# A hybrid decoder step: the clamp of the SSD decay matrix, by eight ScalarE Relus with a bias and a negated Exp

## The chip, the cores and the metric

The program runs on one core of one Trainium2 chip. The metric is the time of one execution on the device in microseconds, the median of several. Five engines work side by side, each with its own queue of instructions that it carries out strictly in order: PE (TensorE, matrix products), DVE (VectorE), ACT (ScalarE), POOL (GpSimd) and SP (SyncE, which here only issues DMAs). They wait for each other by semaphores.

## The reference

One layer with two branches over a prompt of 2048 tokens and a small sample batch: sliding-window attention, and a Mamba-2 state-space scan (SSD). The edited lines belong to the scan of the prompt, in chunks of 128 tokens, 32 heads in 4 groups:

```python
a_cs = jnp.cumsum(dts * A.reshape(SSD_GROUPS, SSD_HPG), axis=2)
seg = a_cs[:, :, :, None] - a_cs[:, :, None]
Lm = jnp.exp(jnp.where(causal[:, :, None, None], seg, -jnp.inf))
cb = jnp.einsum('bclgn,bcsgn->bclsg', Cs, Bs)
y_diag = jnp.einsum('bclsg,bclsgh,bcsghp->bclghp', cb, Lm, dx)
...
y_off = jnp.einsum('bclgn,bcghpn,bclgh->bclghp', Cs, h_prev, jnp.exp(a_cs))
```

`Lm` is the decay matrix of a head: the exponent of the difference of two cumulative sums, for l >= s only. `a_cs` falls along the chunk, so below the diagonal the difference is never positive, and a clamp at zero changes nothing there; above it the clamp keeps the exponent finite, and the product with the masked `cb` makes it zero.

## The kernel before

The kernel has three stages. The first (`phase_t1`) projects q, k, v and does the attention; the second (`phase_s`) is the state-space branch; the third (`phase_t2`) does the output projections, with the sample batch in between. The prompt is cut into four blocks `b` of 512 tokens, each block into four chunks `c` of 128.

In `phase_s` each of the 4 x 4 pairs of block and head group first goes through `proj_group`: ten projections of 24 products each (`L181`, 128x512), which are drained by ACT (`L742`, `L743`) and convolved by DVE (`L748`, three per tile); the weights come by DMA (`raw`), and ACT and DVE split them into a high and a low part (`whl`, `L147`, `L148`). Then `ssd_group` does the scan. For each of its four chunks, with eight heads:

- `AB` is the cumulative sum of the eight heads along the free axis, spread over all partitions by a DMA; `acs` holds the same sums with a token per partition. Line 843, eight times on DVE, one head each, forms `min(AB - acs, 0)` in `L`; line 844 on ACT takes the exponent of all eight; line 845 on POOL multiplies by the masked product `cbm`. `AB` and `L` have two buffers each.
- `EB` is the sum again, spread over half the partitions by two DMAs (`L850`), its exponent taken on ACT (`L851`) and multiplied on DVE (`L855`) by `po`, the product of C with the state `H` (`L854`, on PE).
- PE transposes x (`L858`), DVE scales it twice (`dx`, `wx`, `L861` and `L862`), PE multiplies `dx` by `L` (`py`, `L866`). `wx` is split on ACT and POOL (`ws`, `L868`, `L869`), and PE forms the chunk's state product `st` from it (`L872`, three products).
- POOL decays the state (`hd`, `L878`), DVE adds the new part (`H`, `L879`); the next chunk's `po` needs this `H`. The output is summed by POOL and DVE (`L881`, `L882`, `L884`, `L885`).

After the four chunks the output is squared on ACT (`L887`), summed and split on DVE (`L888` to `L892`, `thl`), and two products on PE (`L895`) give the sums over partitions.

No queue is written out by hand. The framework schedules the whole program at compile time with a cost model of its own and so fixes the order of each engine's instructions: the products of the next group's projections stand between the small products of this group's scan. At run time each engine keeps to that order and waits where its input is late.

Of the kernel before, what the change touches and what calls it, by code (L numbers as in the profile page):

```python
# [11 lines left out]
AF = mybir.ActivationFunctionType  # L12
ALU = mybir.AluOpType
# [62 lines left out]
def build(tc, nc, a, o, seq, phases=("T1", "S", "T2"), dbg=None):  # L76
    NB = seq // TB
    V, A, G, PE, SY = nc.vector, nc.scalar, nc.gpsimd, nc.tensor, nc.sync
# [67 lines left out]
    def split(hi, lo, src, **kw):  # L146
        A.copy(hi, src)  # L147
        V.tensor_tensor(lo, src, hi.bitcast(F32), ALU.subtract)  # L148
# [557 lines left out]
    def phase_s():  # L706
        with ExitStack() as es:
# [115 lines left out]
            def ssd_group(b, g, xT, BT, CT, zs, dt, acs, dec, wd):  # L823
                tr = trp.tile([P, NT, P], F32, name="tr", tag="tr")
                for c in range(NT):
                    PE.transpose(tr[:, c], BT[:, c * P : (c + 1) * P], ident)
                Bt = ck.tile([P, 2, NT, P], F32R, name="Bt", tag="Bt", bufs=1)
                split(Bt[:, 0], Bt[:, 1], tr)
                pcb = trp.tile([P, NT, P], F32, name="tr", tag="tr")
                for c in range(NT):  # L830
                    sl = slice(c * P, (c + 1) * P)
                    PE.matmul(pcb[:, c], BT[:, sl], CT[:, sl], start=True, stop=True)
                cbm = ck.tile([P, NT, P], F32, name="cbm", tag="cbm")
                V.tensor_tensor(cbm, pcb, tri.unsqueeze(1).to_broadcast([P, NT, P]), ALU.mult)  # L834
                for c in range(NT):
                    first = b == 0 and c == 0
                    sl = slice(c * P, (c + 1) * P)
                    hc = slice(c * 32 + 8 * g, c * 32 + 8 * g + 8)
                    AB = lp.tile([P, 8, P], F32, name="AB", tag="AB")
                    SY.dma_start(AB.rearrange("p h l -> p (h l)"), ac_d[b][hc].rearrange("h l -> (h l)").partition_broadcast(P))  # L840
                    L = lp.tile([P, 8, P], F32, name="L", tag="L")
                    for h in range(8):
                        V.tensor_scalar(L[:, h], AB[:, h], acs[:, hc.start + h : hc.start + h + 1], 0.0, ALU.subtract, ALU.min)  # L843
                    A.activation(L, L, AF.Exp)  # L844
                    G.tensor_tensor(L, L, cbm[:, c].unsqueeze(1).to_broadcast([P, 8, P]), ALU.mult)  # L845
                    if not first:
                        EB = lp.tile([P, 4, P], F32, name="EB", tag="EB")
                        for hl in range(2):
                            src = ac_d[b][hc].rearrange("(i l) t -> l i t", l=2)[hl]
                            SY.dma_start(EB[64 * hl : 64 * hl + 64], src.partition_broadcast(64))  # L850
                        A.activation(EB, EB, AF.Exp)  # L851
                        po = yop.tile([P, 4, P], F32, name="po", tag="po")
                        for i in range(4):
                            PE.matmul(po[:, i], H[g][:, i * P : (i + 1) * P], CT[:, sl], start=True, stop=True)  # L854
                        V.tensor_tensor(EB, po, EB, ALU.mult)  # L855
                    tr = trp.tile([P, 8, 64], F32, name="tr", tag="tr")
                    for i in range(4):
                        PE.transpose(tr[:, 2 * i : 2 * i + 2].rearrange("p h d -> p (h d)"), xT[:, i, sl], ident)  # L858
                    dx = ck.tile([P, 8, 64], F32, name="dx", tag="dx")
                    wx = ck.tile([P, 8, 64], F32, name="wx", tag="wx", bufs=1)  # L860
                    V.tensor_tensor(dx, tr, dt[:, hc].unsqueeze(2).to_broadcast([P, 8, 64]), ALU.mult)  # L861
                    V.tensor_tensor(wx, tr, wd[:, hc].unsqueeze(2).to_broadcast([P, 8, 64]), ALU.mult)  # L862
                    py = yp.tile([P, 4, P], F32, name="py", tag="py")
                    for i in range(4):
                        for hl in range(2):
                            PE.matmul(py[64 * hl : 64 * hl + 64, i], dx[:, 2 * i + hl], L[:, 2 * i + hl], start=True, stop=True)  # L866
                    ws = ck.tile([P, 2, 8, 64], F32R, name="ws", tag="ws", bufs=1)
                    A.copy(ws[:, 0], wx)  # L868
                    G.tensor_tensor(ws[:, 1], wx, ws[:, 0].bitcast(F32), ALU.subtract)  # L869
                    pst_ = stp.tile([P, 8, 64], F32, name="st", tag="st")  # L870
                    for n, (x, y) in enumerate(SPLIT3):
                        PE.matmul(pst_, Bt[:, x, c], ws[:, y], start=n == 0, stop=n == 2)  # L872
                    Hg = H[g].rearrange("p (h d) -> p h d", h=8)
                    if first:
                        V.tensor_copy(Hg, pst_)
                    else:
                        hd = ck.tile([P, 8, 64], F32, name="hd", tag="hd", bufs=1)
                        G.tensor_tensor(hd, Hg, dec[:, hc].unsqueeze(2).to_broadcast([P, 8, 64]), ALU.mult)  # L878
                        V.tensor_tensor(Hg, pst_, hd, ALU.add)  # L879
                    u = xT[:, :, sl]  # L880
                    G.tensor_tensor(u, u, Dcol[:, 4 * g : 4 * g + 4].unsqueeze(2).to_broadcast([P, 4, P]), ALU.mult)  # L881
                    V.tensor_tensor(u, py, u, ALU.add)  # L882
                    if not first:
                        G.tensor_tensor(u, u, EB, ALU.add)  # L884
                    V.tensor_tensor(zs[:, :, sl], zs[:, :, sl], u, ALU.mult)  # L885
                SY.dma_start(v_d[b][g].rearrange("c p t -> p c t"), zs)
                A.activation(xT, zs, AF.Square)  # L887
                V.tensor_tensor(xT[:, :2], xT[:, :2], xT[:, 2:], ALU.add)  # L888
                V.tensor_tensor(xT[:, 0], xT[:, 0], xT[:, 1], ALU.add)
                thl = sqp.tile([P, 2, TB], F32R, name="thl", tag="thl")  # L890
                V.tensor_copy(thl[:, 0], xT[:, 0])
                V.tensor_tensor(thl[:, 1], xT[:, 0], thl[:, 0].bitcast(F32), ALU.subtract)  # L892
                pss = stp.tile([32, TB], F32, name="st", tag="st")
                for i in range(2):
                    PE.matmul(pss, onesr, thl[:, i], start=i == 0, stop=i == 1)  # L895
                sm = sqp.tile([1, TB], F32, name="sm", tag="sm")
                A.copy(sm, pss[:1])
                SY.dma_start(ss_d[b][g], sm)
# [8 lines left out]
            for b in range(NB):  # L907
                dts_ = dt_block(b)
                hT = load_h(b, b == sb)
                for g in range(4):  # L910
                    ssd_group(b, g, *proj_group(b, g, hT), *dts_)
                    stats(b, g)
# [404 lines left out]
```

## Time and profile before

| | |
|---|---|
| median of 3 runs | 3275.4 us (3272.0 to 3277.6) |
| span of the profiled execution, first to last instruction | 3273.9 us |
| the median of the runs less that span | 1.5 us |
| PE busy | 3130.4 us, 96% |
| DVE busy | 2234.8 us, 68% |
| ACT busy | 1308.2 us, 40% |
| POOL busy | 1045.0 us, 32% |
| first and last start of line 843 | 850.1 and 2050.3 us |
| first and last start of line 887, once in each of 16 groups | 909.5 and 2064.3 us |

The profile is of one execution, and its own time is the span; what a run spends before the first and after the last instruction is not in it. Busy time of PE is counted to the modelled end of each product, and products overlap, so a busy PE may still do less than its best; a PE that is not busy is waiting. A stretch from one start of line 887 to the next is one group of the SSD stage. The granted clock is the share of full speed that the throttle gave TensorE.

### The profile page before, as it was taken

How to read it: one execution, taken by the hardware profiler on the slowest of the kernel's cores; microseconds unless marked ns; L12 is line 12 of the kernel's file. 1: busy time of each engine (PE TensorE's matmuls, PEld its weight loads, DVE VectorE, ACT ScalarE, POOL GpSimd, SP SyncE). 2: the span in 40 equal slices, each digit the busy share in tenths (PEclk: the TensorE clock that was granted, in tenths of full speed). 3: DMA queues.
4: the chain of work that ended last, by engine and by line, in shares of the span. 5: the costliest groups of instructions: out<-in, count | busy, mean ns of one | idle time of the engine just before them, and what ended most of it. 6: DMA issues, size and time to landing. Idle time of an engine off the chain costs nothing.

```text
span 3273.9 us, 49350 instructions
## 1 busy us (share of the span) xinstructions
PE 3130.4 (96%) x19038; PEld 2656.9 (81%) x19038; DVE 2234.8 (68%) x3777; ACT 1308.2 (40%) x2334; POOL 1045.0 (32%) x965
## 2 busy tenths in 40 slices
PE   6999999999989999998999999999999999999999
PEld 5978787878878877776777777788877799999888
DVE  3777768678887798989888898555555554334433
ACT  3555535456344344434444444332333333222322
POOL 1534343443445455556554555200211110000000
PEclk8999999999999999999999999999999999999999
DMA  6544425323433444444344433444764574345443
GB/s 210 156 134 124 128 73 169 106 70 124 130 122 110 154 125 135 126 156 133 116 143 155 127 118 119 154 141 117 229 184 142 131 226 147 97 135 168 132 116 101
DMA packets 472788, 448.76 MB, mean 137 GB/s; under 512 B 33808, under 2 KB 420520, under 8 KB 472504
## 3 DMA queue, kind: packets, MB, share of 16 engines
q1 hardware_dynamic: 472552, 445.60, 44.9%
q8 instruction: 150, 2.46, 0.3%
q14 instruction: 86, 0.70, 0.1%
HBM read 382.26 MB, written 65.35 MB: 137 GB/s over the span
## 4 chain that ended last, share of the span: by engine, by line
PE 63%; DVE 24%; DMA 5%; POOL 3%; issue 3%; ACT 2%; SPq 1%; DVEq 0%; ACTq 0%; POOLq 0%
PE mm L181 37%; PE mm L192 11%; DVE acc L748 5%; DVE L L843 5%; PE mm L168 5%; DVE whl L148 3%; PE tr L547 3%; PE sc L519 2%; POOL L L845 2%; DVE zs L885 1%; DMA v<-v_d 1%; PE tr L536 1%; DVE xT L882 1%; DVE H L879 1%; DMA hT<-h_d 1%
## 5 line engine op out<-in xcount | busy, mean ns | idle before, releaser
L181 PE MATMUL mm<-hT,whl 128*128 128x512 f32 (+1 forms) x6720 | 1353.7, 357 | 19.8 <-DMA hT<-h_d 9.9
L181 PEld LDWEIGHTS mm<-hT,whl 128*128 128x128 f32 x6720 | 1122.0, 190 | 194.0 <-issue 22.9
L148 DVE TENSOR_TENSOR whl<-raw,whl 128x2048 fp32r<-128x2048 f32 (+1 forms) x232 | 522.7, 2256 | 261.7 <-ACT whl L147 255.4
L181 PE MATMUL mm<-ot,whl 128*128 128x512 f32 (+1 forms) x2880 | 571.7, 356 | 1.2 <-DVE whl L148 0.8
L181 PEld LDWEIGHTS mm<-ot,whl 128*128 128x128 f32 x2880 | 476.1, 189 | 74.0 <-issue 5.7
L147 ACT CAST whl<-raw 128x2048 fp32r<-128x2048 f32 (+1 forms) x232 | 412.7, 1787 | 250.1 <-PE mm L181 133.9
L192 PE MATMUL mm<-whl,hT 128*128 128x256 f32 (+1 forms) x2304 | 305.6, 288 | 16.2 <-ACT whl L147 12.8
L192 PEld LDWEIGHTS mm<-whl,hT 128*128 128x128 f32 x2304 | 288.6, 190 | 24.4 <-ACT whl L147 13.0
L748 DVE SCALAR_TENSOR_TENSOR acc<-cr,cwb,acc 128x512 f32<-128x512 f32 x288 | 274.9, 960 | 10.4 <-ACT acc L743 5.0
L845 POOL TENSOR_TENSOR L<-L,cbm 128x1024 f32<-128x1024 f32 x64 | 200.2, 3138 | 115.3 <-DVE cbm L834 57.9
L192 PE MATMUL mm<-whl,ot 128*128 128x256 f32 (+1 forms) x1632 | 203.9, 284 | 0.0
L192 PEld LDWEIGHTS mm<-whl,ot 128*128 128x128 f32 (+1 forms) x1632 | 197.6, 188 | 5.3 <-issue 4.9
L168 PE MATMUL mm<-hT,whl 128*128 128x512 f32 x768 | 195.1, 403 | 6.0 <-DVE zs L418 3.7
L843 DVE TENSOR_SCALAR L<-AB,acs 128x128 f32<-128x128 f32 x512 | 192.0, 443 | 0.0
L168 PEld LDWEIGHTS mm<-hT,whl 128*128 128x128 f32 x768 | 142.6, 191 | 42.0 <-issue 5.2
L844 ACT ACTIVATE L<-L 128x1024 f32<-128x1024 f32 x64 | 67.8, 1062 | 187.8 <-DVE L L843 187.8
L365 ACT ACTIVATE s<-s,ng 128x128 f32<-128x128 f32 x256 | 100.0, 394 | 59.9 <-DVE ng L359 57.7
L147 ACT CAST ot<-v 128x512 fp32r<-128x512 f32 x96 | 59.0, 621 | 158.4 <-DVE v L1183 79.9
L752 ACT ACTIVATE th<-acc 128x512 f32<-128x512 f32 x96 | 60.6, 632 | 145.4 <-DVE acc L748 145.3
L869 POOL TENSOR_TENSOR ws<-wx,ws 128x512 fp32r<-128x512 f32 x64 | 102.5, 1601 | 44.4 <-ACT ws L868 44.4
L540 POOL TENSOR_TENSOR PT<-PT 128x512 f32<-128x512 f32 x60 | 78.2, 1308 | 92.6 <-DVE PT L539 78.9
L1183 DVE SCALAR_TENSOR_TENSOR v<-v,snw,rb 128x512 f32<-128x512 f32 x64 | 48.0, 770 | 84.7 <-DMA v<-v_d 84.7
(320 smaller groups left out, 3964.3 us busy)
## 6 DMA issues: line engine op xcount, KB each, us to landing
raw<-in_w_in_dram SPq DMA_DIRECT2D x120, 1024.0 KB
hT<-h_d SPq DMA_DIRECT2D x80, 512.0 KB
raw<-in_w_in_dram SPq DMA_DIRECT2D x64, 512.0 KB
AB<-ac_d SPq DMA_DIRECT2D x64, 512.0 KB
raw<-in_w_ssd_proj_dram SPq DMA_DIRECT2D x32, 1024.0 KB
v_d<-zs SPq DMA_DIRECT2D x16, 1024.0 KB
v<-v_d SPq DMA_DIRECT2D x64, 256.0 KB
raw<-in_w_attn_proj_dram SPq DMA_DIRECT2D x64, 256.0 KB
```

What stands on the lines that cost most here:

```text
L147: A.copy(hi, src)
L148: V.tensor_tensor(lo, src, hi.bitcast(F32), ALU.subtract)
L168: PE.matmul(ps, hl[:, x, k, c0 : c0 + P], ht[:, y, :], start=first and i == 0, stop=last and i == n - 1,)
L181: PE.matmul(ps, hl[:, x, k, c0 : c0 + P], ht[:, y, lo : lo + n], start=i == 0, stop=i == 3 * len(hT) - 1,)
L192: PE.matmul(ps, ht[:, x, tt * P : tt * P + m], hl[:, y, k, :n], start=i == 0, stop=i == 3 * len(hT) - 1,)
L365: A.activation(s[:, i, :width], s[:, i, :width], AF.Exp, bias=ng[:, i : i + 1], accum_out=den[:, i : i + 1])
L540: G.tensor_tensor(PT[:, 0], PT[:, 0], PT[:, 1], ALU.subtract)
L547: PE.matmul(po[64 * kvl : 64 * kvl + 64], vT[:, tt + w, kv * HD : (kv + 1) * HD], PTs[kvl][:, w], start=w == ws[0], stop=w == 1,)
L748: V.scalar_tensor_tensor(out=acc, in0=raw[:, k : k + TB], scalar=cwb[:, k, ct : ct + 1], in1=acc, op0=ALU.mult, op1=ALU.add)
L843: V.tensor_scalar(L[:, h], AB[:, h], acs[:, hc.start + h : hc.start + h + 1], 0.0, ALU.subtract, ALU.min)
L845: G.tensor_tensor(L, L, cbm[:, c].unsqueeze(1).to_broadcast([P, 8, P]), ALU.mult)
L869: G.tensor_tensor(ws[:, 1], wx, ws[:, 0].bitcast(F32), ALU.subtract)
```

## The change

The eight instructions of line 843 go from DVE to ACT. Each is a Relu of `-AB + acs`, which is `-min(AB - acs, 0)`, with the column of `acs` as the bias of each partition; the exponent takes the negative by its scale. Nothing else in the source changes.

```diff
--- before.py
+++ after.py
@@ -840,8 +840,8 @@
                     SY.dma_start(AB.rearrange("p h l -> p (h l)"), ac_d[b][hc].rearrange("h l -> (h l)").partition_broadcast(P))
                     L = lp.tile([P, 8, P], F32, name="L", tag="L")
                     for h in range(8):
-                        V.tensor_scalar(L[:, h], AB[:, h], acs[:, hc.start + h : hc.start + h + 1], 0.0, ALU.subtract, ALU.min)
-                    A.activation(L, L, AF.Exp)
+                        A.activation(L[:, h], AB[:, h], AF.Relu, scale=-1.0, bias=acs[:, hc.start + h : hc.start + h + 1])
+                    A.activation(L, L, AF.Exp, scale=-1.0)
                     G.tensor_tensor(L, L, cbm[:, c].unsqueeze(1).to_broadcast([P, 8, P]), ALU.mult)
                     if not first:
                         EB = lp.tile([P, 4, P], F32, name="EB", tag="EB")
```

The scheduler lays the whole SSD stage out anew. Three places show it; all are in the third head group (`H_8613`) of a later block, which repeats almost unchanged from group to group.

The first is on PE, in the middle of a group: from the end of the state product of the first chunk (`st`) to the `po` of the third. `mm` are products of the projections. Before:

```order
L181 MATMUL mm<-hT,whl 128x512 x13
L858 MATMUL tr<-cst,xT 128x128 x4
L866 MATMUL py<-L,dx 64x128 x8
L181 MATMUL mm<-hT,whl 128x512 x5
L854 MATMUL po<-CT,H_8613 128x128 x4
L872 MATMUL st<-ws,Bt 128x512 x3
L181 MATMUL mm<-hT,whl 128x512 x8
L866 MATMUL py<-L,dx 64x128 x8
L181 MATMUL mm<-hT,whl 128x512 x28
L854 MATMUL po<-CT,H_8613 128x128 x4
```

And now:

```order
L181 MATMUL mm<-hT,whl 128x512 x13
L858 MATMUL tr<-cst,xT 128x128 x4
L866 MATMUL py<-L,dx 64x128 x5
L854 MATMUL po<-CT,H_8613 128x128 x4
L866 MATMUL py<-L,dx 64x128 x3
L872 MATMUL st<-ws,Bt 128x512
L181 MATMUL mm<-hT,whl 128x512 x6
L872 MATMUL st<-ws,Bt 128x512 x2
L181 MATMUL mm<-hT,whl 128x512 x16
L866 MATMUL py<-L,dx 64x128 x8
L181 MATMUL mm<-hT,whl 128x512 x8
L854 MATMUL po<-CT,H_8613 128x128 x4
```

Between one chunk's `st` and the next chunk's `po`, which needs the updated `H`, stand fewer products than before: 18 and then 36 before, 13 and then 24 now (the last six products ahead of the rest of `st` are not counted).

The second place is the end of the same group, on PE and on DVE. PE before, from the `st` of the third chunk to the product on `thl`:

```order
L872 MATMUL st<-ws,Bt 128x512 x3
L866 MATMUL py<-L,dx 64x128 x8
L181 MATMUL mm<-hT,whl 128x512 x20
L854 MATMUL po<-CT,H_8613 128x128 x4
L872 MATMUL st<-ws,Bt 128x512 x3
L181 MATMUL mm<-hT,whl 128x512 x66
L895 MATMUL st<-thl,onesr 32x512
```

PE now:

```order
L872 MATMUL st<-ws,Bt 128x512 x3
L181 MATMUL mm<-hT,whl 128x512 x11
L866 MATMUL py<-L,dx 64x128 x8
L181 MATMUL mm<-hT,whl 128x512 x5
L854 MATMUL po<-CT,H_8613 128x128 x4
L872 MATMUL st<-ws,Bt 128x512
L181 MATMUL mm<-hT,whl 128x512 x4
L872 MATMUL st<-ws,Bt 128x512 x2
L181 MATMUL mm<-hT,whl 128x512 x61
L895 MATMUL st<-thl,onesr 32x512
```

From `st` to the fourth `po` there are 16 `mm` in place of 20; from that `po` to `thl` 65 in place of 66.

DVE before, at the same place (`L843` is the edited line, `whl` the split of a weight, `L855` the product with `EB`, `L885` the last sum of a chunk):

```order
L882 TENSOR_TENSOR xT<-py,xT 128x4x128
L843 TENSOR_SCALAR L<-AB,acs 128x128 x8
L748 SCALAR_TENSOR_TENSOR acc<-cr,cwb,acc 128x512
L885 TENSOR_TENSOR zs<-zs,xT 128x4x128
L148 TENSOR_TENSOR whl<-raw,whl 128x2048
L748 SCALAR_TENSOR_TENSOR acc<-cr,cwb,acc 128x512
L753 SCALAR_TENSOR_TENSOR xT<-th,acc 128x512
L855 TENSOR_TENSOR EB<-po,EB 128x512
L879 TENSOR_TENSOR H_8613<-st,hd 128x512
L748 SCALAR_TENSOR_TENSOR acc<-cr,cwb,acc 128x512 x2
L885 TENSOR_TENSOR zs<-zs,xT 128x4x128
```

DVE now:

```order
L882 TENSOR_TENSOR xT<-py,xT 128x4x128
L855 TENSOR_TENSOR EB<-po,EB 128x512
L879 TENSOR_TENSOR H_8613<-st,hd 128x512
L748 SCALAR_TENSOR_TENSOR acc<-cr,cwb,acc 128x512
L885 TENSOR_TENSOR zs<-zs,xT 128x4x128
L748 SCALAR_TENSOR_TENSOR acc<-cr,cwb,acc 128x512
L148 TENSOR_TENSOR whl<-raw,whl 128x2048
L748 SCALAR_TENSOR_TENSOR acc<-cr,cwb,acc 128x512
L888 TENSOR_TENSOR xT<-xT 128x1024
```

The eight of `L843` are gone, and the split `L148` that stood ahead of the last `EB` and `H` now stands behind them and behind `L885`.

The third place is on ACT and on SP, in such a group. ACT before, from the tanh of a convolution (`L752`) to the second exponent (`L844`) after it:

```order
L752 ACTIVATE th<-acc 128x512
L868 CAST ws<-wx 128x512
L844 ACTIVATE L<-L 128x1024
L742 COPY cr<-mm 128x512
L743 ACTIVATE acc<-mm,cwb 128x512
L147 CAST whl<-raw 128x2048
L851 ACTIVATE EB<-EB 128x512
L844 ACTIVATE L<-L 128x1024
```

ACT now:

```order
L752 ACTIVATE th<-acc 128x512
L843 ACTIVATE L<-AB,acs 128x128 x8
L868 CAST ws<-wx 128x512
L844 ACTIVATE L<-L 128x1024
L742 COPY cr<-mm 128x512
L743 ACTIVATE acc<-mm,cwb 128x512
L147 CAST whl<-raw 128x2048
L851 ACTIVATE EB<-EB 128x512
L843 ACTIVATE L<-AB,acs 128x128 x8
L868 CAST ws<-wx 128x512
L844 ACTIVATE L<-L 128x1024
```

The eight Relus stand in a row, ahead of the cast of `ws`, the exponent and the draining of the projections (`L742`, `L743`).

SP before, the loads of one group:

```order
L840 DMA AB<-ac_d_93 128x1024
L850 DMA EB<-ac_d_93 64x4x128 x2
L840 DMA AB<-ac_d_93 128x1024
L154 DMA raw<-in_w_in_dram 128x8x256
L850 DMA EB<-ac_d_93 64x4x128 x2
L840 DMA AB<-ac_d_93 128x1024
L850 DMA EB<-ac_d_93 64x4x128 x2
L840 DMA AB<-ac_d_93 128x1024
L154 DMA raw<-in_w_in_dram 128x8x128 x2
L850 DMA EB<-ac_d_93 64x4x128 x2
L886 DMA v_d_2_82<-zs 128x4x512
```

SP now:

```order
L840 DMA AB<-ac_d_93 128x1024
L850 DMA EB<-ac_d_93 64x4x128 x4
L840 DMA AB<-ac_d_93 128x1024
L154 DMA raw<-in_w_in_dram 128x8x256
L840 DMA AB<-ac_d_93 128x1024
L850 DMA EB<-ac_d_93 64x4x128 x2
L840 DMA AB<-ac_d_93 128x1024
L850 DMA EB<-ac_d_93 64x4x128 x2
L886 DMA v_d_2_82<-zs 128x4x512
L154 DMA raw<-in_w_in_dram 128x8x128 x2
```

The second `AB` of a group now stands behind four `EB` loads, where it stood behind two.

## Rows read from the trace of the kernel before

**Rows 1.** Page, part 1: each engine's busy us, share of the span, instructions.

```profile
PE 3130.4 (96%) x19038; PEld 2656.9 (81%) x19038; DVE 2234.8 (68%) x3777; ACT 1308.2 (40%) x2334; POOL 1045.0 (32%) x965
```

**Rows 2.** Busy us and instructions of each engine by stretch, granted clock, DMA.

```profile
850.00:1147.10 297.10, 273.18 (x1957) 251.88 (x1956) 247.66 (x424) 122.70 (x191) 156.66 (x118) 0.97 0.41 130
1147.10:2064.30 917.20, 845.33 (x4482) 680.85 (x4481) 814.17 (x1159) 398.12 (x503) 500.48 (x399) 0.98 0.43 132
1304.60:1379.30 74.70, 70.65 (x380) 57.01 (x379) 67.65 (x96) 33.66 (x43) 41.12 (x34) 1.00 0.42 127
1379.30:1470.90 91.60, 83.32 (x421) 67.39 (x420) 75.74 (x110) 37.96 (x50) 42.03 (x35) 0.94 0.47 153
2001.50:2064.30 62.80, 50.42 (x282) 40.10 (x281) 49.72 (x63) 24.14 (x31) 34.36 (x22) 0.92 0.37 114
```

**Rows 3.** Waits of PE, 850 to 2064.3 us: total us, times, longest.

```profile
PE po L854 <- DVE H L879: 37.4, 29, 4.2
PE st L895 <- DVE thl L891: 14.3, 9, 2.5
PE py L866 <- DVE xT L882: 9.5, 9, 2.1
PE mm L181 <- DMA hT<-h_d: 7.4, 2, 3.8
PE st L872 <- POOL ws L869: 6.8, 13, 1.4
PE tr L858 <- DVE Bt L148: 4.3, 1, 4.3
...
PE mm L181 <- DVE whl L148: 3.8, 2, 3.0
```

**Rows 4.** Waits of PE in the group from 1304.6 us.

```profile
PE st L895 <- DVE thl L891: 1.5, 1, 1.5
PE po L854 <- DVE H L879: 1.4, 2, 1.1
PE py L866 <- DVE xT L882: 0.9, 1, 0.9
PE st L872 <- POOL ws L869: 0.3, 1, 0.3
```

**Rows 5.** Timeline of DVE in that group: start us, us, line, operation, operands.

```profile
1338.98 3.75 DVE L843 TENSOR_SCALAR L<-AB,acs 128x128 f32<-128x128 f32 x8
...
1343.85 0.67 DVE L879 TENSOR_TENSOR H<-st,hd 128x512 f32<-128x512 f32 x1
...
1357.58 3.92 DVE L843 TENSOR_SCALAR L<-AB,acs 128x128 f32<-128x128 f32 x8
...
1368.08 1.84 DVE L843 TENSOR_SCALAR L<-AB,acs 128x128 f32<-128x128 f32 x8
...
1371.10 2.28 DVE L148 TENSOR_TENSOR whl<-raw,whl 128x2048 fp32r<-128x2048 f32 x1
```

**Rows 6.** Busy us of line 843 alone, by stretch.

```profile
850.00:2064.30 1214.30, 192.05 (x512) 0.98 0.42 132
1304.60:1379.30 74.70, 11.33 (x32) 1.00 0.42 127
```

**Rows 7.** Timeline of PE: an unbroken run of products of that group.

```profile
1367.57 15.14 PE L181 MATMUL mm<-hT,whl 128*128 128x512 f32 x66
```

**Rows 8.** Timeline of ACT in the attention stage, softmax exponents.

```profile
400.67 0.39 ACT L365 ACTIVATE s<-s,ng 128x128 f32<-128x128 f32 x1
400.96 0.19 ACT L365 ACTIVATION_READ_ACCUMULATOR s<-s,ng 128x1 f32 x1
```

**Rows 9.** Page, part 5: busy, mean ns | idle before, releaser.

```profile
L845 POOL TENSOR_TENSOR L<-L,cbm 128x1024 f32<-128x1024 f32 x64 | 200.2, 3138 | 115.3 <-DVE cbm L834 57.9
```

**Rows 10.** Line 845: ns least/median/most, first and last start us.

```profile
L845 POOL TENSOR_TENSOR L<-L,cbm x64: 2342/2435/5287, 856.0 to 2051.8; 128x1024 f32<-128x1024 f32 x64
```

**Rows 11.** Waits of the SP queue, 850 to 2064.3 us.

```profile
SPq L850 <- POOL xT L884: 177.5, 39, 13.4
```

## The prediction

> **What bounds the kernel now.** First the page's line of busy shares: PE is busy 96% of the span, so whatever is done to another engine can only pay where PE still stands still [rows 1]. Next a table of stretches. The instructions of the diff lie between 850 and 2064 us, the SSD phase. There PE is busy 273.18 of 297.1 us and 845.33 of 917.2 us: it stands still for 23.9 + 71.9 = 95.8 us, while DVE is busy 83 to 89% and ACT 41 to 43% [rows 2]. In the undisturbed groups, as in the one from 1304.6 us on (74.7 us; five of the twelve later groups have this length to a microsecond), PE is busy 70.65 us, DVE 67.65, POOL 41.12 and ACT 33.66 [rows 2]. So PE is the bound, and 4.05 us of each such group are lost to waits.
>
> Then the waits of PE in this phase. The five largest that end with a DVE instruction are the state update H (L879) 37.4, the split of the squares thl (L891) 14.3, the output sum xT (L882) 9.5, and 4.3 and 3.8: 69.3 us of the 95.8 [rows 3]. Two others are no matter of DVE: the load of the next block's hT, 7.4, and POOL's ws, 6.8 [rows 3]. The undisturbed group shows the same on a small scale: 1.5 for thl, 1.4 for H, 0.9 for xT, 0.3 for ws [rows 4].
>
> Why DVE is late is in its timeline. The eight subtract-min instructions take 1.84 us at best and 3.75 or 3.92 us at other times, and the H update of the chunk stands a few places behind them (1343.85 after the eight that began at 1338.98) [rows 5]. A last piece is the clock: PE ran at a granted 0.94 in two stretches and at 0.92 in the last one, against 1.00 in the undisturbed group [rows 2].
>
> **What the change removes.** 512 DVE instructions, 64 times eight, that hold DVE for 192.05 us of the phase and for 11.33 us of an undisturbed group [rows 6]. DVE would be busy 56.3 of 74.7 us, 75% in place of 91%. None of these microseconds counts by itself; what counts is how much of the 69.3 us of PE waiting goes.
>
> The order answers that with the durations. PE's own instructions keep their number, but the new order draws the chunks of a group together. A product of 512 columns costs PE 15.14 / 66 = 0.23 us from start to start [rows 7]. From the state product of chunk 1 to the po of chunk 2 there were 18 such products and eight py; now 13 and five, which leaves the H update some 1.5 us less. Chunk 2 to 3: 36 before, 24 after, 2.8 us less. Chunk 3 to 4: 20 before, 16 after, 0.9 less. On the other side the H update of chunk 1 comes 3.75 us earlier, that of chunk 3 3.92 earlier [rows 5]. So the waits for H (1.4) and xT (0.9) have 2 to 3 us of reserve after the change. The way to thl begins with the po of chunk 4. PE does 66 products between the two before and 65 after, so its room stays. On DVE the eight (1.84 us from 1368.08) and a weight split (2.28 us from 1371.10) stood ahead of that chunk's EB product [rows 5]; in the new order the eight are gone and the weight split stands behind the last sum, L885. That is 4 us for a wait of 1.5, which should go too. In an undisturbed group all 3.8 us of DVE waits [rows 4] could so disappear. The block boundaries and the first block are less regular and have the longer waits, so for the whole phase I let one fifth stay: **55 us of the 69.3 go**. Bounds: none of it (DVE was not the cause) to all 69.3.
>
> **What it adds.** 512 Relus on ACT. There is none of this shape and operand kinds in the SSD phase before; the nearest row is the softmax exponent, 128x128 with a per-partition bias: 0.39 us long, and the next instruction starts 0.29 us after its start [rows 8]. Eight cost 7 x 0.29 + 0.39 = 2.4 us; without any overlap 8 x 0.39 = 3.1; were the operation free it would be 0. I take 2.4, since eight stand in a row in the order. That is 9.7 us in a group and 155 us in all, on an engine that was busy 33.66 of 74.7 us: 43.4, or 58% [rows 2]. So it lies beside PE's work. The Exp keeps its length: the scale of -1 changes a constant. What queues behind the Relus on ACT: the cast ws, the Exp itself and the draining of the convolution's PSUM tiles (L742, L743); they come up to 2.4 us later at four places of a group, while three PSUM tiles of 24 products, 5.5 us each, stand between that and PE. I put 0.5 us of new PE waiting per group on this.
>
> The multiplication by the masked product on POOL (L845) is the next in the chain. Its median is 2.44 us, its mean 3.14 [rows 9, 10], so 0.7 us of delay on average is already in it. Since the chunks are closer together, POOL has less room: between chunk 3's and chunk 4's L845 the new order has a multiplication, an addition and the split of ws, where two multiplications stood. I put another 0.5 us per group on POOL. Both together, 16 groups x 1.0 = **16 us come back**. Bounds 0 to 30.
>
> The AB and EB loads are the same DMAs; their order on SP changes (rival three). Phase one before 850 us and the last phase after 2064 us keep their order and hold none of the edited instructions: 0.
>
> **Clock.** 91.6 us at 0.94, once more a stretch of 91 us like it, 62.8 us at 0.92 and the first block's 297.1 us at 0.97 are 5.5 + 5.5 + 5.0 + 8.9 = 25 us of work lost against full speed [rows 2]. The two stretches at 0.94 hold the waits for hT, which no edit touches; of the remaining 14 us I let half come back, **7 us**, because the long DVE-ended waits before them get shorter. Bounds 0 to 14.
>
> **Sum.** -55 + 16 - 7 = -46 us against a span of 3273.9 us: 3228. The time of a run includes a little outside the span; the median of the runs shown is 3275.4, 1.5 us above, so I carry the difference over: **3229 us**, 1.4% faster. Its own bounds: half of the DVE waits go and 30 come back (-35 + 30 = -5, 3270) to -69 - 14 = -83 (3192); the likely part of that is 3203 to 3262.
>
> **Rivals.**
>
> *The waits only change owner.* PE is bound by an order laid down in advance; the new one leaves the chunk chain less room, and POOL takes DVE's place as the one that is late. For it: L845's mean is 0.7 us over its median, and from the state product of chunk 1 to that of chunk 4 there are now 63 of the 512-column products and were 74, so 2.5 us less [rows 7, 9, 10]. If each of these three steps waits for POOL by 0.7, and a fifth of the DVE waits (0.8) stays, a group loses 2.9 + ACT's 0.5 = 3.4 of the former 4.05. 16 x 0.65 = 10 us: 3265. Against it: in the whole phase PE waited only 6.8 us for POOL's ws [rows 3]. Chance 0.17.
>
> *PE runs without gaps.* All waits but hT's go (95.8 - 7.4 = 88) and 14 us of clock come back: 3275 - 102 = 3173. For it: DVE falls to 75%, with room everywhere. Against it: ACT and POOL get less room than they had. Chance 0.09.
>
> *ACT becomes the late one, slower.* ACT works strictly in order. Before, no ACT instruction waited for AB; now the first of each eight does, with the PSUM draining behind it. And on SP the second AB load of a group now stands behind four EB loads, not two. These wait for POOL to release EB, with a longest wait of 13.4 us [rows 11]. A Relu group that stands d us for AB once in a group delays everything on ACT by d; the PSUM tiles and the room between py of chunk 1 and py of chunk 3 absorb about 5 us of it. With d = 10 in each group PE loses 5 us, 16 x 5 = 80, against 46 saved: 3309. It decides against the change from d = 8 on. Against it: there are two AB buffers, so a load has about two chunks' time from release to use; between the eights that began at 1338.98 and 1357.58 lie 18.6 us [rows 5]. Chance 0.13. In a sentence of its own: the Trainium skill, page "ScalarE: Activation LUTs", section "Rules for kernel authors", says to use VectorE and not ScalarE for relu, min and add; in the terms of this kernel that means eight instructions of 2.4 us for eight of 1.84, and if all 64 chains lay on PE's path the time would be 64 x 0.6 = 38 us longer, 3314, inside this rival. The trace speaks against it here, since the engine that PE waits for is DVE and ACT has more than half of its time free.
>
> **How the numbers follow.** Forecast 0.61 (3203 to 3262), change of owner 0.17, no gaps 0.09, ACT late 0.13. About 0.2% is what a measurement of this kernel can tell from no change, here 6.6 us: faster ends at 3268.8. The change of owner, 3265 with some ten on either side, gives 0.07 faster and 0.10 the same. Faster: 0.61 + 0.09 + 0.07 = 0.77; the same 0.10; slower 0.13. The range 3188 to 3280 leaves out ACT's case and most of the case without gaps, about 0.2.
>
> **What would show it.** In the profile after: DVE busy near 56 us in an undisturbed group of 71 to 72.5 us, PE's waits for H and xT nearly gone and thl's under 1 us; ACT busy near 43; the Relus 0.3 us apart. The forecast is wrong if the group stays at 74 us with the waits at POOL's L845 or ws, or if PE's waits for ACT's L743 (and ACT's for AB) come up to several us in each group.

## The result, and the profile after

The changed kernel takes 3219.6 us (median of four runs, 3214.5 to 3225.5), the kernel before 3273.95 us beside it (four runs): 54 us less, ratio 0.9837 with a 95% interval of [0.9825, 0.9848]. The forecast was 3229 us, 46 us less, with a range of 3188 to 3280: the sign, the main mechanism and the size held, the terms inside the sum less well.

The page of the changed kernel: the span, the busy time of each engine, and the rows of the Relus and of POOL's multiplication (busy us, mean ns | idle before, releaser).

```profile
span 3217.3 us, 49376 instructions
...
PE 3120.6 (97%) x19038; PEld 2653.4 (82%) x19038; DVE 2092.4 (65%) x3265; ACT 1453.1 (45%) x2846; POOL 1059.3 (33%) x965
...
L845 POOL TENSOR_TENSOR L<-L,cbm 128x1024 f32<-128x1024 f32 x64 | 184.4, 2891 | 104.7 <-DVE cbm L834 101.8
...
L843 ACT ACTIVATE L<-AB,acs 128x128 f32<-128x128 f32 x512 | 156.8, 389 | 31.1 <-PE py L866 22.8
```

The 512 instructions have changed engine: DVE has 142 us less, ACT 145 us more [rows 1]. PE, with the same 19038 products, is busy 9.8 us less and stands still for 3217.3 - 3120.6 = 96.7 us, where it stood for 143.5. So 46.8 us of the gain are waits that went and 9.8 us are products that took less time; together they are the 56.6 us between the two spans.

Stretches of the changed kernel, with the columns of [rows 2]: the first block, the other twelve groups, the rest of the program, an undisturbed group and the last one.

```profile
850.00:1120.60 270.60, 259.91 (x1924) 241.34 (x1924) 211.72 (x288) 160.51 (x333) 150.85 (x117) 0.99 0.44 139
1120.60:2001.20 880.60, 845.66 (x4510) 684.67 (x4509) 707.21 (x781) 503.44 (x871) 520.23 (x400) 0.99 0.44 138
2001.20:3217.30 1216.10, 1206.36 (x7204) 1050.43 (x7202) 571.67 (x935) 366.63 (x514) 74.21 (x62) 0.99 0.50 148
1564.60:1637.20 72.60, 70.68 (x380) 57.30 (x379) 59.01 (x64) 42.82 (x76) 43.12 (x35) 1.00 0.42 131
1932.20:2001.20 69.00, 61.21 (x324) 49.31 (x323) 47.05 (x50) 29.40 (x48) 37.62 (x25) 0.92 0.37 115
```

The SSD phase is 63.1 us shorter: 26.5 in the first block, 36.6 in the twelve groups [rows 2]. PE's idle time in it falls from 95.8 us to 10.7 + 34.9 = 45.6. What follows the phase is 6.5 us longer (1209.6 before): PE is busy 3.8 us more there, with four products more inside the window and a clock of 0.99 in place of 1.00, and waits 2.7 us more. An undisturbed group takes 72.6 us in place of 74.7, with the same 380 products.

The waits of PE in the phase (total us, times, longest), and in that undisturbed group:

```profile
PE py L866 <- DVE xT L882: 10.0, 8, 1.3
PE po L854 <- DVE H L879: 9.3, 15, 1.6
PE st L872 <- POOL ws L869: 5.7, 6, 1.5
PE tr L858 <- DVE cbm L834: 4.7, 1, 4.7
PE mm L181 <- DMA hT<-h_d: 3.8, 2, 2.4
PE mm L181 <- DVE whl L148: 3.3, 2, 3.0
PE mm L181 <- ACT acc L743: 2.7, 2, 2.2
PE py L866 <- POOL L L845: 1.8, 2, 1.2
...
PE st L895 <- DVE thl L891: 0.5, 1, 0.5
```

```profile
PE py L866 <- DVE xT L882: 1.2, 1, 1.2
PE po L854 <- DVE H L879: 0.6, 1, 0.6
```

Against [rows 3]: H falls from 37.4 to 9.3, thl from 14.3 to 0.5, xT stays (9.5, now 10.0), whl stays (3.8, now 3.3), Bt is gone and a wait of nearly its length for cbm stands in its place. In the group [rows 4] thl is gone, H is down from 1.4 to 0.6, xT up from 0.9 to 1.2.

ACT, first what the Relus cost and what they waited for (ns least/median/most; idle us, times), then one chunk in the timeline (start us, us):

```profile
L843 ACT ACTIVATE L<-AB,acs x512: 383/388/414, 849.4 to 1986.4; 128x128 f32<-128x128 f32 x171
...
  PE py L866: 22.8, 8
  DMA AB<-ac_d: 4.5, 4
```

```profile
1616.98 2.44 ACT L843 ACTIVATE L<-AB,acs 128x128 f32<-128x128 f32 x8
1619.32 0.60 ACT L868 CAST ws<-wx 128x512 fp32r<-128x512 f32 x1
1619.83 1.06 ACT L844 ACTIVATE L<-L 128x1024 f32<-128x1024 f32 x1
```

Eight Relus take 2.44 us, and the cast and the exponent follow at once. The wait for AB that the slower rival was built on comes four times, 4.5 us in all. The 22.8 us for `py` are ACT waiting for an L that PE still reads: there ACT is early, not late.

### The profile page after: what moved, and what is told of

It reads as the page before. It is cut to its first block, busy times and chain, and to the rows that moved or that the text cites. A ratio compares the mean times of both kernels' runs of the same rounds, so it can differ in the third digit from the quotient of the medians.

```text
span 3217.3 us, 49376 instructions
## 1 busy us (share of the span) xinstructions
PE 3120.6 (97%) x19038; PEld 2653.4 (82%) x19038; DVE 2092.4 (65%) x3265; ACT 1453.1 (45%) x2846; POOL 1059.3 (33%) x965
## 4 chain that ended last, share of the span: by engine, by line
PE 71%; DVE 13%; POOL 6%; DMA 5%; issue 3%; ACT 2%; SPq 1%; DVEq 0%; POOLq 0%; ACTq 0%
PE mm L181 45%; PE mm L192 10%; PE mm L168 5%; DVE acc L748 3%; PE tr L547 3%; POOL L L845 2%; DVE whl L148 2%; PE sc L519 2%; POOL ws L869 1%; PE tr L536 1%; DVE zs L885 1%; POOL xT L884 1%; DMA xt<-in_x_prompt_dram 1%; POOL hd L878 1%; DMA v<-v_d 1%
## 5 line engine op out<-in xcount | busy, mean ns | idle before, releaser
L148 DVE TENSOR_TENSOR whl<-raw,whl 128x2048 fp32r<-128x2048 f32 (+1 forms) x232 | 527.0, 2275 | 262.9 <-ACT whl L147 262.5
L748 DVE SCALAR_TENSOR_TENSOR acc<-cr,cwb,acc 128x512 f32<-128x512 f32 x288 | 286.3, 997 | 15.4 <-POOL L L845 8.0
L845 POOL TENSOR_TENSOR L<-L,cbm 128x1024 f32<-128x1024 f32 x64 | 184.4, 2891 | 104.7 <-DVE cbm L834 101.8
L843 ACT ACTIVATE L<-AB,acs 128x128 f32<-128x128 f32 x512 | 156.8, 389 | 31.1 <-PE py L866 22.8
L814 ACT ACTIVATE th<-mm 128x512 f32<-128x512 f32 (+1 forms) x80 | 40.2, 511 | 158.7 <-PE mm L181 152.2
L1175 ACT ACTIVATE t<-mm 128x512 f32<-128x512 f32 (+1 forms) x76 | 37.6, 518 | 162.5 <-PE mm L181 141.2
L752 ACT ACTIVATE th<-acc 128x512 f32<-128x512 f32 x96 | 60.5, 630 | 109.0 <-DVE acc L748 108.9
L884 POOL TENSOR_TENSOR xT<-xT,EB 128x512 f32<-128x512 f32 x60 | 90.8, 1514 | 50.9 <-DVE EB L855 34.0
## 6 DMA issues: line engine op xcount, KB each, us to landing
v<-v_d SPq DMA_DIRECT2D x64, 256.0 KB
raw<-in_w_attn_proj_dram SPq DMA_DIRECT2D x64, 256.0 KB
```

The source lines that it names most:

```text
L748: V.scalar_tensor_tensor(out=acc, in0=raw[:, k : k + TB], scalar=cwb[:, k, ct : ct + 1], in1=acc, op0=ALU.mult, op1=ALU.add)
L843: A.activation(L[:, h], AB[:, h], AF.Relu, scale=-1.0, bias=acs[:, hc.start + h : hc.start + h + 1])
```

## Experiments

The theory under test: PE waited for DVE, and the gain is DVE's lighter load. Its rivals: the new order of instructions alone does it; the Relus' time on ACT, or ACT's late results, take part of it back. The kernel before took 3274 to 3275 us beside each of these runs. Medians, with the ratio to the kernel before and DVE's and ACT's busy time on the profile's page:

| kernel | us | ratio [95%] | DVE busy | ACT busy |
|---|---|---|---|---|
| before | 3274 | 1 | 2234.8 | 1308.2 |
| dve_ballast | 3281.4 | 1.0022 [1.0012, 1.0033] | 2237.2 | 1453.6 |
| half | 3261.9 | 0.9961 [0.9949, 0.9974] | 2194.0 | 1386.5 |
| dve_one | 3236.4 | 0.9882 [0.9862, 0.9901] | 2160.4 | 1304.5 |
| no_clamp | 3227.6 | 0.9848 [0.9825, 0.9871] | 2101.7 | 1303.6 |
| relu_twice | 3226.6 | 0.9849 [0.9831, 0.9867] | 2090.7 | 1620.5 |
| after_again | 3219.6 | 0.9826 [0.9809, 0.9843] | 2093.0 | 1452.7 |
| wx_act | 3202.4 | 0.9781 [0.9767, 0.9795] | 2079.9 | 1553.5 |
| dcol_act | 3195.1 | 0.9756 [0.9743, 0.9769] | 2074.8 | 1526.3 |
| both_act | 3195.7 | 0.9759 [0.9746, 0.9772] | 2049.6 | 1623.9 |

**after_again**, the changed kernel itself on another occasion.

> The changed kernel unchanged, on the same chip as the three beside it, so that steps of less than one per cent can be compared. 3215 to 3225.

The two measurements agree, 0.9837 and 0.9826 with overlapping intervals.

**dve_ballast**: the changed kernel, with the old work put back on DVE for nothing.

```diff
+J = lp.tile([P, P], mybir.dt.bfloat16, name="J", tag="J", bufs=1)
+for h in range(8):
+    V.tensor_scalar(J, AB[:, h], acs[:, hc.start + h : hc.start + h + 1], 0.0, ALU.subtract, ALU.min)
```

> The changed kernel, and in addition the eight subtract-min instructions of each chunk on DVE again, with a result that nobody reads (written in 16 bits to a scratch tile). ACT carries the Relus all the same. Theory (DVE's load is what matters): most of the 54 us is lost again, 3255 to 3280. Rival (the gain is the scheduler's new order, or the chain through L that no longer passes DVE's queue, and not the load): 3219 to 3235.

The whole gain is gone; the kernel is 0.22% slower than before, 1 us past the range of the theory. Its order on PE is laid out anew once more, but is still drawn together (in most groups 13 products between the first `st` and the next `po`, where there were 18), and its ACT still does the Relus. The load is back (first row, from the page) and the wait for H with it (second, PE's waits in the phase):

```profile
L847 DVE TENSOR_SCALAR J<-AB,acs 128x128 bf16<-128x128 f32 x512 | 216.9, 424 | 18.5 <-DMA AB<-ac_d 13.7
```

```profile
PE po L857 <- DVE H L882: 32.7, 15, 4.1
```

So with DVE's load back, a drawn-together order and an L that no longer passes DVE's queue give nothing: DVE's load is the cause.

**no_clamp**: neither engine clamps.

```diff
-for h in range(8):
-    A.activation(L[:, h], AB[:, h], AF.Relu, scale=-1.0, bias=acs[:, hc.start + h : hc.start + h + 1])
-A.activation(L, L, AF.Exp, scale=-1.0)
+A.activation(L, AB, AF.Exp)
```

> The clamp is left out on both engines: the exponent reads AB itself, so L holds other values. DVE is relieved as in the changed kernel, and ACT does not get the 512 Relus. Theory (the gain is PE no longer waiting for a late DVE; the Relus are hidden beside PE): 3205 to 3218, at most 15 us below the changed kernel's 3219.6. Rival (ACT pays back a good part of what DVE gives): 3170 to 3195.

It missed the expectation on the slow side: without any Relu the kernel is no faster than with them (0.9848 against 0.9837 and 0.9826). 150 us of ACT work bring no gain when they go. The order was laid out anew for this kernel too, and PE's waits fell elsewhere:

```profile
PE st L893 <- DVE thl L889: 14.8, 12, 2.4
```

thl, which the change had brought to 0.5 us, is back at 14.8, while H and xT are lower (6.0 and 6.1 for 9.3 and 10.0); in all PE stands still for 51.3 us in the phase where it stood for 45.6. Two kernels with nearly the same load on DVE (2101.7 and 2092.4 us) thus differ by 8 us, and these runs can't say how much of that is the order. So a cost of ACT below some 8 us can't be seen by comparing them.

**relu_twice**: every Relu done twice on ACT, the first time into a scratch tile.

```diff
+for h in range(8):
+    A.activation(J, AB[:, h], AF.Relu, scale=-1.0, bias=acs[:, hc.start + h : hc.start + h + 1])
```

> The changed kernel with each Relu done twice, the first time into a scratch tile that nobody reads: 157 us more on ACT, which would be busy about 53 of 72.6 us in an undisturbed group. Theory (ACT has room beside PE): 3220 to 3235. Rival (ACT is close to the bound, its queue holds up the drains of PE's PSUM tiles): 3250 to 3300.

167 us more on ACT cost 7 us by the medians, and the intervals overlap. PE's wait for `ws`, whose first half ACT casts behind the Relus, rises from 5.7 to 13.2 us, and the wait of `py` for xT leaves the list. With no_clamp on the other side, the bound on ACT's part is this: with none, one or two sets of Relus the medians stay within 3220 to 3228 us.

**dve_one**: the kernel before, with one subtract-min of 1024 elements in place of eight; the first head's bias serves all eight heads.

```diff
-for h in range(8):
-    V.tensor_scalar(L[:, h], AB[:, h], acs[:, hc.start + h : hc.start + h + 1], 0.0, ALU.subtract, ALU.min)
+V.tensor_scalar(L, AB, acs[:, hc.start : hc.start + 1], 0.0, ALU.subtract, ALU.min)
```

> The kernel before, with one subtract-min of 1024 elements in place of the eight of 128, with the bias of the first head for all heads, so that L holds other values. DVE does the same elements, but has an eighth of the instructions, and ACT gets nothing. Theory (DVE's time counts, however it is saved; eight of 1.84 to 3.9 us become one of about 0.6 to 1.5): 3215 to 3240. Rival (it must be another engine, since DVE's place in the chain is what holds PE up): 3262 to 3274.

As expected: the clamp stays on DVE, ACT gets nothing, and 74 us less on DVE bring 38 of the 54 us. So it isn't the change of engine that pays, but the time DVE no longer spends. Here some of the waits do change owner: POOL's `ws` is now PE's longest, 17.1 us for 6.8 before.

**half**: four heads on DVE, four on ACT.

```diff
+for h in range(4):
+    V.tensor_scalar(L[:, h], AB[:, h], acs[:, hc.start + h : hc.start + h + 1], 0.0, ALU.subtract, ALU.min)
-for h in range(8):
+for h in range(4, 8):
     A.activation(L[:, h], AB[:, h], AF.Relu, scale=-1.0, bias=acs[:, hc.start + h : hc.start + h + 1])
-A.activation(L, L, AF.Exp, scale=-1.0)
+A.activation(L[:, :4], L[:, :4], AF.Exp)
+A.activation(L[:, 4:], L[:, 4:], AF.Exp, scale=-1.0)
```

> Four heads of each chunk stay on DVE as subtract-min with an exponent of their own, four go to ACT as Relus with the negated exponent. Theory (DVE's load sets PE's waits, in proportion while DVE is near its limit; ACT's load sets none): about half of the gain or a little more, 3232 to 3248. Rival (the first relief of DVE already gives everything, since after it other waits hold PE): 3217 to 3228.

Both expectations missed: half of the instructions bring 13 us, a quarter of the gain. DVE's busy time fell by only 41 us, and the table of DVE's lines in the phase says where the rest stayed:

```profile
L843 DVE TENSOR_SCALAR L<-AB,acs 128x128 f32<-128x128 f32 x256 | 151.8, 649 | 0.0
```

Half of the 192.05 us [rows 6] would be 96; 151.8 are left, or 593 ns of DVE for each of the 256 where it was 192.05 / 512 = 375. The timeline of DVE and POOL in this kernel shows what stretches it (L843 is the clamp, L848 POOL's multiplication):

```profile
1267.04 1.19 DVE L843 TENSOR_SCALAR L<-AB,acs 128x128 f32<-128x128 f32 x4
...
1272.81 3.00 POOL L848 TENSOR_TENSOR L<-L,cbm 128x1024 f32<-128x1024 f32 x1
1272.82 0.74 DVE L748 SCALAR_TENSOR_TENSOR acc<-cr,cwb,acc 128x512 f32<-128x512 f32 x1
...
1274.68 3.65 DVE L843 TENSOR_SCALAR L<-AB,acs 128x128 f32<-128x128 f32 x4
1275.78 1.26 POOL L887 TENSOR_TENSOR xT<-xT,EB 128x512 f32<-128x512 f32 x1
1277.00 1.04 POOL L881 TENSOR_TENSOR hd<-H,dec 128x512 f32<-128x512 f32 x1
...
1278.24 0.68 DVE L753 SCALAR_TENSOR_TENSOR CT<-th,acc 128x512 f32<-128x512 f32 x1
```

The same four clamps take 1.19 us in one place and 3.65 us beside POOL's instructions at 1272.81, 1275.78 and 1277.00: the first three end 0.1 us after POOL's next instruction begins, each in 1.1 to 1.3 us, the fourth takes 0.28. What eight clamps cost was in good part POOL's time, and four clamps that meet the same POOL instructions wait as long. In the whole trace 106 of the 256 clamps take over 0.5 us; in the kernel before it was 96 of the 512.

**wx_act**: the changed kernel, with `wx` (L862) scaled on ACT, head by head.

```diff
-V.tensor_tensor(wx, tr, wd[:, hc].unsqueeze(2).to_broadcast([P, 8, 64]), ALU.mult)
+for h in range(8):
+    A.activation(wx[:, h], tr[:, h], AF.Identity, bias=0.0, scale=wd[:, hc.start + h : hc.start + h + 1])
```

> The changed kernel, and the scaling wx (L862, one DVE instruction of 0.68 us per chunk) as eight ACT instructions of 64 columns. DVE loses another 38 us, ACT gains about 100 us, which fits into the room that the doubled Relus showed. Theory (DVE-ended waits, still some 31 us, shrink further): 3205 to 3217. Rival (the eight small instructions sit in the chain wx, ws, st, and PE waits for ws instead): 3222 to 3245.

17 us faster than the changed kernel, a little more than expected. But DVE's busy time falls by 13 us only, not by the expected 38: the 43.5 us of the line are gone, and other lines are longer (L148 214.1 us in the phase for 198.8, L748 276.9 for 267.5). ACT pays 111 us for the eight times 64 columns:

```profile
L863 ACT ACTIVATE wx<-tr,wd 128x64 f32<-128x64 f32 x512 | 111.4, 327 | 80.4 <-DVE dx L861 50.7
```

**dcol_act**: the changed kernel, with the skip product x D (L881) moved from POOL to ACT.

```diff
-G.tensor_tensor(u, u, Dcol[:, 4 * g : 4 * g + 4].unsqueeze(2).to_broadcast([P, 4, P]), ALU.mult)
+for i in range(4):
+    A.activation(u[:, i], u[:, i], AF.Identity, bias=0.0, scale=Dcol[:, 4 * g + i : 4 * g + i + 1])
```

> The changed kernel, and the product of x with the skip weight (L881, one POOL instruction of 1.0 to 1.5 us per chunk) as four ACT instructions of 128 columns. POOL loses about 78 us and ACT gains about 80. Theory (POOL and DVE lengthen each other where they run at the same time; the L748 and L885 that took 2.3 and 2.9 us in place of 0.7 stand beside POOL work): DVE's mean L748 falls below its 997 ns and the time to 3205 to 3217. Rival (what is left of PE's waits comes from the order, not from POOL): 3217 to 3228.

The best result, 24.5 us under the changed kernel and beyond what was expected. The sign named for it hardly came: L748's mean is 988 ns on the page against 997, 288 x 9 ns = 2.6 us. Yet DVE is busy 17.6 us less with the same 3265 instructions, in other lines: in the phase the sum of L885 (L886 in this kernel) goes from 78.8 to 70.5 us and that of L148 from 198.8 to 190.0. PE's waits in the phase:

```profile
PE mm L181 <- DMA hT<-h_d: 6.9, 2, 3.9
PE st L872 <- POOL ws L869: 3.9, 5, 1.4
PE po L854 <- DVE H L879: 3.0, 4, 0.9
...
PE py L866 <- DVE xT L883: 0.5, 1, 0.5
```

The waits for xT (10.0) and H (9.3) went for the most part, and the one for cbm (4.7) is gone. How much of that is POOL's lighter load in itself, and how much the shorter way from POOL's product to DVE's sum L882 (now L883) that it shortens too, and how much the new order, these runs don't tell apart.

**both_act**: both edits together.

> The changed kernel with two further parts moved to ScalarE together: the scaling of wx (eight VectorE-side column scalings per chunk become eight ScalarE Identities) and the skip product x times D (from GpSimd to four ScalarE Identities per chunk). Theory: each takes away other waits of TensorE (the one 17 us, the other 25 us under the changed kernel's time), but only some 25 us of waits in the SSD phase are left behind the second, 7 of them for DMA; a part of the first one's gain is left to win: 3180 to 3193 us, with ScalarE at about 1620 us busy. Rival: what is left is TensorE's own work, or ScalarE with both loads becomes the late engine in each chunk: 3193 to 3215 us, with waits for ScalarE on top of TensorE's list.

The time is the rival's: DVE is 25 us lighter than in dcol_act, and the ratio is the same (0.9759 and 0.9756, intervals overlapping). Its sign, ACT at the top of PE's list, didn't come: PE's waits in the phase are small and have many owners, ACT among them:

```profile
PE st L897 <- DVE thl L893: 3.8, 2, 3.5
PE tr L858 <- DVE xT L753: 3.4, 2, 1.7
...
PE mm L181 <- ACT acc L743: 3.0, 3, 1.6
```

Over half of them still end with DVE (15.5 us of 28.0), but less busy time on DVE no longer shortens the kernel. dcol_act alone, the simpler edit, is the version to keep: 3195 us, 2.4% under the kernel before.

## Why the prediction was right

| term | forecast | measured |
|---|---|---|
| PE's waits that end with DVE | -55 | -44 |
| PE's waits that end with ACT and POOL | +16 | -3 |
| PE's waits for the load of hT | 0 | -4 |
| clock | -7 | -9.8 (PE busy, same products) |
| phases one and three | 0 | +3.4 idle |
| sum | -46 | -56.6 in the spans, -54 in the medians |

The first three rows come from the whole lists of waits: those that end with DVE are 74.8 us before and 30.8 after, with ACT and POOL 13.0 and 10.2, with hT 7.4 and 3.8. Together they fall by 50.4 us; PE's idle time by the stretches says the same (95.8 to 45.6).

**What bounds the kernel** held: PE stays the bound, and most of what was to be had were its waits. dve_ballast shows the cause named, DVE's load, and dve_one shows it from the other side.

**The DVE term was too large by 11 us.** The five waits of the forecast fell from 69.3 to 23.1 us, two thirds and not four fifths, and a new one of 4.7 (cbm) came. The step that was mis-sized stands in "DVE would be busy 56.3 of 74.7 us": it is 59.01 of 72.6. Of the 192 us of line 843, DVE's load in the phase fell by 1061.8 - 918.9 = 143 only. The remainder went into other lines, as the last section shows. Of the signs named, xT was to be "nearly gone" and stayed (10.0 us), while thl went almost entirely (0.5). The undisturbed group, 72.6 us, is just past the 71 to 72.5 forecast.

**Nothing came back on ACT and POOL.** The 0.5 us per group was 8 us for each. PE's waits that end with ACT fell, from 6.0 to 2.7 us; the times of no_clamp and relu_twice alone couldn't have told 8 us from nothing. PE's waits for POOL rose by 0.5 us in all: those for ws fell from 6.8 to 5.7, those for L rose from 0.2 to 1.8. The reasoning took the shorter chain for less room. But POOL gets its input earlier (L845 waited 57.4 us for the exponent before and 2.9 after), and L845's mean fell from 3138 [rows 9] to 2891 ns. POOL as a whole wasn't relieved: with the same 517 instructions it is busy 671.1 us in the phase for 657.1, L878 for one 89.0 for 75.0. The two errors, -44 for -55 and -3 for +16, go in opposite directions; that the sum came within 8 us is in part luck.

**The Relus' price** was right: 2.44 us per eight for 2.4 forecast, 9.75 us in the group, 42.82 us of ACT there for 43.4.

**The clock** gave 9.8 us for 7, but in good part not where the forecast had it: 12.9 us less busy time in the phase, of which the last stage takes 3.8 back at 0.99. The forecast held the two stretches at 0.94 fixed, since they hold the waits for hT, "which no edit touches", and let half of the rest return. Here are the second of those stretches before (the first is in [rows 2]) and both of them in the changed kernel:

```profile
1692.90:1783.80 90.90, 82.83 (x418) 67.24 (x417) 74.78 (x105) 38.06 (x49) 44.16 (x36) 0.94 0.49 154
```

```profile
1342.60:1426.40 83.80, 80.90 (x429) 66.25 (x428) 67.43 (x82) 45.77 (x83) 43.81 (x37) 1.00 0.56 178
1637.20:1719.50 82.30, 77.72 (x408) 63.38 (x407) 64.66 (x71) 45.48 (x80) 44.66 (x37) 0.98 0.53 173
```

They run at 1.00 and 0.98 and are 7.8 and 8.6 us shorter. PE stood still in each for some 8 us before, for 2.9 and 4.6 after, and the wait for hT itself fell from 3.8 and 3.6 to 1.4 and 2.4 us. Full speed is 2.4 GHz, the other level is 1.2, and a mean such as 0.94 is a stretch with a part at the lower one. Counted as in the forecast, some 9 of the 11 us of work lost there came back. The last group of the phase, from which some was to return, still runs at 0.92 in both kernels; the first block rose from 0.97 to 0.99. That the term came near is in part luck, and why hT arrived in better time isn't shown.

**The rivals.** Change of owner: PE's waits for POOL's L and ws are 7.5 us in all, after 7.0, so it fell. PE without gaps: 45.6 us of gaps are left in the phase. ACT late: relu_twice doubles the load that it needed and loses 7 us by the medians. The rule quoted beside it, the Trainium skill, page "ScalarE: Activation LUTs", section "Rules for kernel authors" (VectorE, not ScalarE, for relu, min and add), is about the price of one operation, and there the trace agrees only for eights that nothing holds up (2.44 against 1.84 us): over the phase eight clamps held DVE for 192.05 / 64 = 3.0 us and eight Relus ACT for 156.8 / 64 = 2.45. For the time of this kernel it points the wrong way, since what decides is which engine PE waits for.

## What to carry to other kernels

Before moving work off an engine, read which engine ends the waits of the one that bounds the kernel; work on an engine with room costs little, as 145 us more on ACT cost nothing here that PE's waits show, and another 167 us there 7 us by the medians. Price the gain by the waits, not by the busy time removed: 192 us of instructions were worth 54. Where DVE and POOL share the work, look at the mean against the least of each line; taking half of a group of instructions away can free far less than half, 41 of 192 us here, if their cost is that they stand beside POOL.

## What the runs showed of the hardware

DVE and POOL hold each other up, and only some instructions are touched. From the table of DVE's lines in the phase of the changed kernel (busy us, mean ns | idle before):

```profile
L885 DVE TENSOR_TENSOR zs<-zs,xT 128x512 f32<-128x512 f32 x64 | 78.8, 1232 | 14.2 <-POOL xT L884 14.2
...
L862 DVE TENSOR_TENSOR wx<-tr,wd 128x512 f32<-128x512 f32 x64 | 43.5, 680 | 23.3 <-POOL ws L869 22.9
L882 DVE TENSOR_TENSOR xT<-py,xT 128x512 f32<-128x512 f32 x64 | 43.4, 678 | 15.7 <-issue 14.3 <-PE py L866 1.3
```

All three are 128x512 tensor-tensor operations. The two that read a product of PE (`tr`, `py`) from PSUM take 680 ns on average; the one with both operands in SBUF takes 1232. In the kernel before it took 991:

```profile
L885 DVE TENSOR_TENSOR zs<-zs,xT 128x512 f32<-128x512 f32 x64 | 63.4, 991 | 0.7 <-POOL xT L884 0.7
```

Together with L748 (256.0 to 267.5 us), L753 (44.3 to 51.8) and L148 (194.7 to 198.8), such lines took over 38 of the 49 us that the change did not free. In the timeline of the changed kernel:

```profile
1612.49 2.41 POOL L845 TENSOR_TENSOR L<-L,cbm 128x1024 f32<-128x1024 f32 x1
1612.57 0.69 DVE L862 TENSOR_TENSOR wx<-tr,wd 128x512 f32<-128x512 f32 x1 [2.17 <-POOL ws L869]
1613.18 2.27 DVE L748 SCALAR_TENSOR_TENSOR acc<-cr,cwb,acc 128x512 f32<-128x512 f32 x1
1614.85 1.50 POOL L881 TENSOR_TENSOR xT<-xT,Dcol 128x512 f32<-128x512 f32 x1
...
1621.89 2.84 POOL L845 TENSOR_TENSOR L<-L,cbm 128x1024 f32<-128x1024 f32 x1
1622.40 2.88 DVE L885 TENSOR_TENSOR zs<-zs,xT 128x512 f32<-128x512 f32 x1
1624.70 1.49 POOL L878 TENSOR_TENSOR hd<-H,dec 128x512 f32<-128x512 f32 x1
1625.21 0.68 DVE L862 TENSOR_TENSOR wx<-tr,wd 128x512 f32<-128x512 f32 x1
```

L862 runs at full pace beside L845. L748 and L885 end 0.6 us after POOL's next instruction begins, as if they had begun their work only when L845 was done; and that next instruction of POOL is itself longer (1.49 us for L878, which takes 1.04 at best, as the same multiplication does at 1277.00 in the rows of half). The Trainium skill, page "SBUF — State Buffer", section "SBUF: two separate sides", says that a DVE instruction in a two-port mode or with two inputs in SBUF and an instruction of GpSimd take an exclusive lock on a shared pair of ports for the whole instruction, and that the other one is blocked; these rows agree. That a lock is the cause, and which other instructions of DVE take it, no run here shows.
